# Tree attention over 96 heads: more heads of Q and K laid side by side by GpSimd, with its queue reordered

## The chip, the cores and the metric

The kernel runs on one core of one Trainium2 chip. The metric is device time in microseconds, the median of three runs, and for each profiled kernel one execution was also recorded in full. PE is TensorE's matmul, PEld its weight load, DVE is VectorE, ACT ScalarE, POOL GpSimd, SP SyncE; L364 is line 364 of the kernel.

## The reference, cut to what matters

Batch 8 and 12 heads give 96 heads, each with 512 queries and keys of 64 numbers. A query attends to its own node of a binary tree and to that node's ancestors.

```python
for i in range(seq):
    mask[i, i] = 1
    parent = i
    while parent > 0:
        parent = (parent - 1) // 2
        mask[i, parent] = 1

scores = np.einsum('bhqd,bhkd->bhqk', Q, K) * scale
scores = scores + (1 - mask) * (-1e9)
weights = np.exp(scores - np.max(scores, axis=-1, keepdims=True))
weights = weights / (np.sum(weights, axis=-1, keepdims=True) + 1e-10)
return np.einsum('bhqk,bhkd->bhqd', weights, V).astype(np.float32)
```

## The kernel before

Heads are worked two at a time: 48 pairs, `i` from 0 to 47. Q and K are loaded in blocks of 8 heads (`KB`), V in blocks of 16 (`VB`, called `o` in the code), each load turning fp32 into bf16 on the way. All these loads and most stores are issued by POOL, in the order in which `pool_program` lists them; a store of the last four heads is issued by SP. Each transfer on POOL's queue takes one of eight semaphores in turn, so that POOL waits at an issue until the transfer eight before it has landed.

The first 16 heads use a narrow layout, the other 80 a wide one. In the wide layout a step of K or Q turns two pairs at once: PE transposes 8 slots (`turn_slot`) into PSUM (`ktp`, `qtp`), and DVE copies the result to `kq` (L470, L474, L478 for K, L493 for Q). Where a block is *laid*, POOL has first copied it (`lay`, L433, two copies of 128x512 a block, one for each turn) into `besideK` or `besideQ`, with the two pairs' halves beside each other, and PE needs one transpose a slot (L441). Where it isn't, PE makes two transposes of 64 columns a slot (L450). There is one `besideK` and one `besideQ`, so a lay has to wait for the turn of the laid block before it. `LAID` names the blocks that are laid.

For each pair PE makes scores by matmuls of mask codes and of keys and queries (L511, L519, L544, L554), ACT takes exponentials (L529, L560), PE multiplies them with V (`values`, L605), and DVE divides by the row sums (`norm`, L651 and L653) into the output tile `of`. V has to be rearranged from its load `vst` into three tiles `vt` by copies of 32 to 128 partitions (`spread`, L364). The parts have names: 6 to 9 are the four copies of V's upper rows into `vt0` (`spread_top` when POOL makes all four), X, N, Z0 and Z1 are others from the same rows, A, B, C and E come from the leaves. `BY_VECTOR` and `BY_SCALAR` list which of them DVE and ACT make at which `i`, and `pool_program` lists POOL's.

`store_rows` *deals* the store of the first heads: instead of one store of 128 partitions it issues four, of 85, 2, 34 and 7 partitions (`DEALT`).

`ready` says from which `i` an entry of `pool_program` may be recorded; for a lay it is the turn of the block before in the program. POOL runs its instructions strictly in the recorded order, so what stands behind a waiting one waits too.

Of the kernel before, what the change touches and what calls it, by code (L numbers as in the profile page):

```python
# [119 lines left out]
def kernel(  # L120
# [7 lines left out]
    nc = tc.nc  # L128
# [7 lines left out]
    WIDE = 8  # L136
    KB, VB, VO = 8, 16, 16
    EIGHT = 2
    LAID = (8, 9, 10, 11)
    assert NH % VB == 0  # L140

    fp32 = mybir.dt.float32
# [280 lines left out]
    def slots(st, i):  # L423
        return st[2 * i // KB].rearrange("p (g x) t d -> p g (x t) d", x=2)

    def lay(name, b):

        st = {"kst": ksts, "qst": qsts}[name][b]
        assert all((name, h) in issued for h in range(KB * b, KB * b + KB))
        laid[name, b] = two = beside[name[0].upper()]  # L430
        for g in range(KB // 4):
            src = st[:, 4 * g:4 * g + 4, :, :].rearrange("p (a x) t d -> p (x t) a d", x=2)
            nc.gpsimd.tensor_copy(  # L433
                out=two[:, g, :, :, :].bitcast(int32), in_=src.bitcast(int32)
            )
# [156 lines left out]
    def values(i):  # L592

        if i < NP - 1:
            obs[i] = ob = psO.tile([P, 2, 512], fp32, name="ob")
        else:
            obs[i] = ob = psS.tile([P, 2, 512], fp32, name="s1")
        e1, e2, vt = ets[i], e2s[i % NE], vts[(head(i, 0) // VB) % NV]

        vtile = VTILE if i < WIDE else WVTILE  # L600
        parts = EIGHT_PARTS if head(i, 0) >= VB * EIGHT else PARTS[i >= WIDE]
        assert all(("vt", n, head(i, a)) in issued for n in parts for a in range(2))

        def product(e, a, t, tile_v, lo=0, hi=128, **flags):
            nc.tensor.matmul(  # L605
                out=ob[lo:hi, a, 65 * t:65 * t + 65],
                lhsT=e[:, a, PLACE[t], lo:hi],
                rhs=vt[vtile[tile_v][0]][:, head(i, a) % VB, vtile[tile_v][1], 0:D + 1],
                **flags,
            )  # L610

        def firsts(a):
            for t in range(4):
                product(e1, a, t, 0, start=t == 0, stop=False)

        def halves(a, last=True):
            for t in (0, 1):
                product(e2, a, t, 1 + SELF[t], 0, 64, start=False, stop=last and t == 1)
                product(e2, a, t, 1 + t, 64, 128, start=False, stop=last and t == 1)

        def wholes(a, last=False):
            for t in (2, 3):
                product(e2, a, t, 1 + t, start=False, stop=last and t == 3)

        if i == NP - 1:
            for a in range(2):
                firsts(a)
                wholes(a)
                halves(a)
        elif i >= 4 * LAID[0] - 4:  # L630
            for a in range(2):
                firsts(a)
            for a in range(2):
                halves(a, False)
            for a in range(2):
                wholes(a, True)
        else:
            for a in range(2):
                firsts(a)
                wholes(a)  # L640
            for a in range(2):
                halves(a)
# [28 lines left out]
    def store_rows(j0, j1):  # L671

        for j in range(j0, j1):
            store(nc.gpsimd, 0, 4, 1, DEALT[j], DEALT[j + 1])

    def pool_program():

# [3 lines left out]
            (load_q, 8, 4), (load_v, 8, 8), (load_k, 12, 4),  # L681
            (load_q, 12, 4), (load_k, 16, 8), (load_q, 16, 4), (load_rows, 1, "upper"),
            (load_rows, 1, "even"), (load_rows, 1, "odd"), (load_q, 20, 4),
            (load_k, 24, 8), (load_q, 24, 8), (load_rows, 2, "upper"),
            (load_k, 32, 8), (load_leaves, 2, 0), (load_leaves, 2, 1),
            (load_q, 32, 8), (load_rows, 3, "upper"),
            (spread_pool, (1, "Z0", 8, 16), (1, "Z1", 8, 16)),
            (load_k, 40, 8), (load_q, 40, 8), (load_leaves, 3, 0), (load_leaves, 3, 1),
            (spread_top, 2, 0, 16), (spread_pool, (2, "Z0", 0, 16), (2, "Z1", 0, 16)),
            (load_q, 48, 8), (spread_pool, (2, "X", 0, 16)),  # L690
            (load_k, 48, 8), (spread_pool, (2, "N", 0, 16)),
            (load_rows, 4, "upper"), (spread_top, 3, 0, 16),
            (load_k, 56, 8), (load_q, 56, 8), (load_leaves, 4, 0), (load_leaves, 4, 1),
            (spread_pool, (3, "X", 0, 16), (3, "N", 0, 16), (3, "Z0", 0, 16), (3, "Z1", 0, 16)),
            (load_k, 64, 8), (store_rows, 0, 2), (load_q, 64, 8), (store_rows, 2, 4),
            (load_k, 72, 8), (spread_top, 4), (store, nc.gpsimd, 4, 12), (lay, "kst", 8),
            (load_q, 72, 8), (spread_pool, (4, "X", 0, 16), (4, "N", 0, 16)),
            (lay, "qst", 8), (load_rows, 5, "upper"),
            (spread_pool, (4, "Z0", 0, 16), (4, "Z1", 0, 16)),
            (load_leaves, 5, 0), (load_leaves, 5, 1), (load_k, 80, 8), (load_q, 80, 8),  # L700
            (store, nc.gpsimd, 16, 8), (lay, "kst", 9), (load_k, 88, 8), (load_q, 88, 8),
            (lay, "qst", 9), (store, nc.gpsimd, 24, 8), (store, nc.gpsimd, 32, 16),
            (spread_top, 5), (lay, "kst", 10), (store, nc.gpsimd, 48, 16), (lay, "qst", 10),
# [43 lines left out]
    for o in range(EIGHT, NH // VB):  # L747
# [15 lines left out]
    }  # L763

    def spread_by(copy, table, i):

# [90 lines left out]
```

## Time and profile before

| | us |
|---|---|
| median of three runs (lowest, highest) | 133.66 (133.48, 133.95) |
| the profiled execution's own time | 133.8 |
| its span, from the first to the last instruction | 131.9 |

The engine times of the page count instructions, not waits. Issuing a transfer is an instruction of its queue; a transfer's time to landing includes all that is queued ahead of it. GB/s counts what was written, so a load of fp32 that lands as bf16 counts half of what it read.

| engine | busy us | share of the span |
|---|---|---|
| PE | 114.7 | 87% |
| DVE | 108.8 | 82% |
| ACT | 94.4 | 72% |
| POOL | 87.1 | 66% |

### The profile page before, as it was taken

To read this page: it belongs to the slowest core of one execution; us is meant where nothing else is said; L and a number is where in the kernel's file an instruction comes from. 1 tells how busy PE (TensorE), PEld (TensorE's weight loads), DVE (VectorE), ACT (ScalarE), POOL (GpSimd) and SP (SyncE) were. 2 spreads that over 40 slices of the span, in tenths; PEclk is the share of its full clock that TensorE was granted. 3 is DMA by queue.
4 is the path that set the end of the run, shared out by engine and by line. 5 is a ranking of instruction groups with operands and counts; after the bars stand their busy time and mean duration, and the time that the engine had idled before them with its cause. 6 is when DMAs were issued, how large, how long until landed. Compare 5 with 4: busy or idle time off the path is not lost.

```text
span 131.9 us, 5281 instructions
## 1 busy us (share of the span) xinstructions
PE 114.7 (87%) x2286; PEld 80.4 (61%) x2289; DVE 108.8 (82%) x261; ACT 94.4 (72%) x153; POOL 87.1 (66%) x118
## 2 busy tenths in 40 slices
PE   6883999999789699899899999999988999999920
PEld 2351576676566476666577677677765766776610
DVE  3438569988999989989999999999999999877350
ACT  4358268989768957968858787787868668688900
POOL 6994624245623998799951899999999977802200
PEclk9999599999999999999999999999999999999996
DMA  3999999999999999999999999999999999999984
GB/s 122 216 190 196 198 199 205 199 199 207 206 200 205 204 202 208 209 202 205 202 208 204 244 236 305 338 204 207 203 288 285 228 391 406 400 402 402 397 315 148
DMA packets 29719, 32.28 MB, mean 245 GB/s; under 512 B 1488, under 2 KB 26704, under 8 KB 29696
## 3 DMA queue, kind: packets, MB, share of 16 engines
q0 software_dynamic: 28416, 30.68, 115.2%
q1 hardware_dynamic: 864, 0.93, 2.1%
q10 hardware_dynamic: 416, 0.33, 1.0%
q8 instruction: 18, 0.29, 0.8%
q14 instruction: 5, 0.04, 0.1%
HBM read 37.96 MB, written 12.58 MB: 383 GB/s over the span
## 4 chain that ended last, share of the span: by engine, by line
DVE 38%; PE 24%; DMA 14%; POOL 10%; issue 5%; ACT 3%; ACTq 1%; POOLq 0%
DVE of L653 12%; DVE vt L364 11%; DMA kst<-in_K_dram 8%; PE ob L605 8%; DMA qst<-in_Q_dram 6%; POOL vt L364 5%; DVE rec L651 3%; PE s L511 3%; DVE kq L493 3%; DVE kq L470 3%; DVE kq L478 3%; DVE kq L474 3%; PE s L519 2%; ACT e L560 2%; PE s L544 1%
## 5 line engine op out<-in xcount | busy, mean ns | idle before, releaser
L529 ACT ACTIVATE e<-s 128x1024 bf16<-128x1024 f32 x40 | 40.9, 1023 | 20.7 <-PE s L519 20.1
L605 PE MATMUL ob<-vt,e 128*128 128x65 bf16 (+1 forms) x940 | 39.8, 198 | 6.0 <-DVE of L653 3.0
L605 PEld LDWEIGHTS <-e 128*128 128x128 bf16 (+1 forms) x960 | 31.7, 103 | 15.9 <-DVE of L653 5.1
L560 ACT ACTIVATE e<-s 128x384 bf16<-128x384 f32 x80 | 34.7, 491 | 0.0
L653 DVE TENSOR_TENSOR of<-ob,rec 128x512 f32<-128x512 f32 x47 | 32.5, 691 | 1.6
L364 POOL COPY vt<-vst 32x512 int32<-32x512 int32 (+1 forms) x38 | 31.0, 816 | 2.9 <-PE ob L605 1.2
L364 DVE COPY vt<-vst 32x1024 bf16<-32x1024 bf16 (+6 forms) x54 | 26.8, 497 | 2.3 <-DMA vst<-in_V_dram 1.3
L662 POOL DMA_DIRECT2D out_dram<-of x13 | 12.1, 928 | 12.7 <-DVE of L653 9.2
L511 PE MATMUL s<-codes 40*128 40x512 bf16 x96 | 19.3, 398 | 0.7 <-ACT e L525 0.4
L519 PE MATMUL s<-kq 64*128 64x512 bf16 x96 | 18.5, 380 | 0.0
L651 DVE RECIPROCAL rec<-ob 128x8 f32<-128x8 f32 x47 | 9.6, 204 | 8.8 <-PE ob L605 8.0
L554 PEld LDWEIGHTS <-kq 64*128 64x128 bf16 x320 | 12.1, 94 | 4.8
L554 PE MATMUL s<-kq 64*128 64x160 bf16 (+1 forms) x320 | 14.6, 208 | 0.0
L544 PE MATMUL s<-codes 40*128 40x384 bf16 x80 | 13.6, 333 | 0.3
L493 DVE COPY kq<-qtp 128x1024 bf16<-128x1024 bf16 x20 | 13.6, 681 | 0.0
L256 POOL DMA_DIRECT2D qst<-in_Q_dram x11 | 8.3, 752 | 6.8 <-DMA vst<-in_V_dram 2.6
L525 ACT ACTIVATE e<-s 128x1024 bf16<-128x1024 f32 x8 | 8.2, 1022 | 6.0 <-PE s L519 5.9
L544 PEld LDWEIGHTS <-codes 40*128 40x128 bf16 x80 | 6.1, 94 | 7.9 <-issue 1.2
L256 POOL DMA_DIRECT2D kst<-in_K_dram x10 | 7.6, 760 | 3.9 <-PE ob L605 2.8
L470 DVE COPY kq<-ktp 128x256 bf16<-128x256 bf16 x20 | 8.3, 415 | 0.3 <-PE ktp L450 0.3
L474 DVE COPY kq<-ktp 128x256 bf16<-128x256 bf16 x20 | 8.3, 415 | 0.0
L478 DVE COPY kq<-ktp 128x512 bf16<-128x512 bf16 x20 | 8.3, 414 | 0.0
(49 smaller groups left out, 139.4 us busy)
## 6 DMA issues: line engine op xcount, KB each, us to landing
kst<-in_K_dram POOLq DMA_DIRECT2D x10, 512.0 KB, 13.2
out_dram<-of POOLq DMA_DIRECT2D x5, 1024.0 KB, 13.9
qst<-in_Q_dram POOLq DMA_DIRECT2D x9, 512.0 KB, 14.5
out_dram<-of POOLq DMA_DIRECT2D x2, 2048.0 KB, 20.8
vst<-in_V_dram POOLq DMA_DIRECT2D x12, 256.0 KB, 14.9
vst<-in_V_dram POOLq DMA_DIRECT2D x6, 512.0 KB, 14.3
out_dram<-of POOLq DMA_DIRECT2D x1, 1536.0 KB, 10.7
qst<-in_Q_dram POOLq DMA_DIRECT2D x5, 256.0 KB, 11.9
```

The costliest lines, as they stand in the source:

```text
L256: return nc.gpsimd.dma_start(out=kept[b][:, h0 % KB:h0 % KB + n, :, :].rearrange("p (g x) t d -> p g (x t d)", x=2), in_=wide[:, h0 // 2:( ...
L364: return copy(out=dst, in_=src)
L493: nc.vector.tensor_copy(out=qq[:, :, 0:16, :].rearrange("p b u c -> p b (u c)"), in_=halves)
L511: nc.tensor.matmul(out=sp[:, a, :], lhsT=(k1code if i < WIDE else k1wide)[64 * a:64 * a + CODE_ROWS, :], rhs=(q1code[64 * a:64 * a + CODE_ ...
L519: nc.tensor.matmul(out=sp[:, a, :], lhsT=keys(i, a, TOP), rhs=qTs[i][64 * a:64 * a + 64, :, :].rearrange("p t c -> p (t c)"), start=False, ...
L529: ) if i < WIDE else nc.scalar.activation(
L544: nc.tensor.matmul(out=flat[:, a, :, :].rearrange("p u (t c) -> p u t c", t=4)[:, :, :, 16:64], lhsT=k2wide[64 * a:64 * a + CODE_ROWS, :], ...
L554: nc.tensor.matmul(out=flat[:, a, :, lo:hi], lhsT=keys(i, a, WTILE2[t]), rhs=qT[64 * a:64 * a + 64, :, lo:hi], start=False, stop=t == 1, s ...
L560: nc.scalar.activation(out=e2s[i % NE][:, a, :, 32:128].rearrange("p t (r u) -> p t r u", u=2), in_=flat[:, a, :, :].rearrange("p u (t r) ...
L605: nc.tensor.matmul(out=ob[lo:hi, a, 65 * t:65 * t + 65], lhsT=e[:, a, PLACE[t], lo:hi], rhs=vt[vtile[tile_v][0]][:, head(i, a) % VB, vtile ...
L651: nc.vector.reciprocal(out=rec[:, a:a + n, :, :], in_=o4[:, a:a + n, :, D:D + 1])
L653: nc.vector.tensor_tensor(out=ofs[g][:, first:last + 1:step, :, :], in0=o4[:, a:a + n, :, 0:D], in1=rec[:, a:a + n, :, :].to_broadcast([P, ...
```

## The change

`LAID` gets blocks 2, 3, 4, 5 and 7 (heads 16 to 47 and 56 to 63) beside 8 to 11; block 6 stays as it is. `lay` can make one of its two copies alone. The order of products in `values` was bound to `LAID` and is now bound to `LATE`, with the same value, 28. The four copies of V's upper rows for heads 32 to 63 (`o` of 2 and 3) go from POOL to ACT, one a step, at steps 12 to 15 and 18 to 21. The dealt store holds heads 0 to 2, and the store behind it 13 heads instead of 12. POOL's list is written anew.

```diff
--- before.py
+++ after.py
@@ -136,7 +136,8 @@
     WIDE = 8
     KB, VB, VO = 8, 16, 16
     EIGHT = 2
-    LAID = (8, 9, 10, 11)
+    LAID = (2, 3, 4, 5, 7, 8, 9, 10, 11)
+    LATE = 28
     assert NH % VB == 0
 
     fp32 = mybir.dt.float32
@@ -423,12 +424,12 @@
     def slots(st, i):
         return st[2 * i // KB].rearrange("p (g x) t d -> p g (x t) d", x=2)
 
-    def lay(name, b):
+    def lay(name, b, g0=0, g1=2):
 
         st = {"kst": ksts, "qst": qsts}[name][b]
-        assert all((name, h) in issued for h in range(KB * b, KB * b + KB))
+        assert all((name, h) in issued for h in range(KB * b + 4 * g0, KB * b + 4 * g1))
         laid[name, b] = two = beside[name[0].upper()]
-        for g in range(KB // 4):
+        for g in range(g0, g1):
             src = st[:, 4 * g:4 * g + 4, :, :].rearrange("p (a x) t d -> p (x t) a d", x=2)
             nc.gpsimd.tensor_copy(
                 out=two[:, g, :, :, :].bitcast(int32), in_=src.bitcast(int32)
@@ -627,7 +628,7 @@
                 firsts(a)
                 wholes(a)
                 halves(a)
-        elif i >= 4 * LAID[0] - 4:
+        elif i >= LATE:
             for a in range(2):
                 firsts(a)
             for a in range(2):
@@ -671,7 +672,7 @@
     def store_rows(j0, j1):
 
         for j in range(j0, j1):
-            store(nc.gpsimd, 0, 4, 1, DEALT[j], DEALT[j + 1])
+            store(nc.gpsimd, 0, 3, 1, DEALT[j], DEALT[j + 1])
 
     def pool_program():
 
@@ -681,23 +682,26 @@
             (load_q, 8, 4), (load_v, 8, 8), (load_k, 12, 4),
             (load_q, 12, 4), (load_k, 16, 8), (load_q, 16, 4), (load_rows, 1, "upper"),
             (load_rows, 1, "even"), (load_rows, 1, "odd"), (load_q, 20, 4),
-            (load_k, 24, 8), (load_q, 24, 8), (load_rows, 2, "upper"),
-            (load_k, 32, 8), (load_leaves, 2, 0), (load_leaves, 2, 1),
-            (load_q, 32, 8), (load_rows, 3, "upper"),
-            (spread_pool, (1, "Z0", 8, 16), (1, "Z1", 8, 16)),
-            (load_k, 40, 8), (load_q, 40, 8), (load_leaves, 3, 0), (load_leaves, 3, 1),
-            (spread_top, 2, 0, 16), (spread_pool, (2, "Z0", 0, 16), (2, "Z1", 0, 16)),
-            (load_q, 48, 8), (spread_pool, (2, "X", 0, 16)),
+            (load_k, 24, 8), (load_q, 24, 8), (load_rows, 2, "upper"), (lay, "kst", 2),
+            (load_k, 32, 8), (lay, "qst", 2, 0, 1), (load_leaves, 2, 0), (load_leaves, 2, 1),
+            (load_q, 32, 8), (lay, "qst", 2, 1, 2), (load_rows, 3, "upper"),
+            (spread_pool, (1, "Z0", 8, 16), (1, "Z1", 8, 16)), (lay, "kst", 3),
+            (load_k, 40, 8), (load_q, 40, 8), (lay, "qst", 3),
+            (load_leaves, 3, 0), (load_leaves, 3, 1), (lay, "kst", 4),
+            (spread_pool, (2, "Z0", 0, 16), (2, "Z1", 0, 16), (2, "X", 0, 16)),
+            (load_q, 48, 8), (lay, "qst", 4),
             (load_k, 48, 8), (spread_pool, (2, "N", 0, 16)),
-            (load_rows, 4, "upper"), (spread_top, 3, 0, 16),
-            (load_k, 56, 8), (load_q, 56, 8), (load_leaves, 4, 0), (load_leaves, 4, 1),
+            (load_rows, 4, "upper"), (lay, "kst", 5),
+            (load_k, 56, 8), (load_q, 56, 8), (lay, "qst", 5),
+            (load_leaves, 4, 0), (load_leaves, 4, 1),
             (spread_pool, (3, "X", 0, 16), (3, "N", 0, 16), (3, "Z0", 0, 16), (3, "Z1", 0, 16)),
-            (load_k, 64, 8), (store_rows, 0, 2), (load_q, 64, 8), (store_rows, 2, 4),
-            (load_k, 72, 8), (spread_top, 4), (store, nc.gpsimd, 4, 12), (lay, "kst", 8),
-            (load_q, 72, 8), (spread_pool, (4, "X", 0, 16), (4, "N", 0, 16)),
-            (lay, "qst", 8), (load_rows, 5, "upper"),
+            (load_k, 64, 8), (store_rows, 0, 2), (load_q, 64, 8), (store_rows, 2, 3),
+            (lay, "kst", 7), (store_rows, 3, 4),
+            (load_k, 72, 8), (load_q, 72, 8), (lay, "qst", 7), (spread_top, 4),
+            (store, nc.gpsimd, 3, 13), (spread_pool, (4, "X", 0, 16)), (load_rows, 5, "upper"),
+            (lay, "kst", 8), (spread_pool, (4, "N", 0, 16)), (lay, "qst", 8),
+            (load_leaves, 5, 0), (load_leaves, 5, 1), (load_k, 80, 8), (load_q, 80, 8),
             (spread_pool, (4, "Z0", 0, 16), (4, "Z1", 0, 16)),
-            (load_leaves, 5, 0), (load_leaves, 5, 1), (load_k, 80, 8), (load_q, 80, 8),
             (store, nc.gpsimd, 16, 8), (lay, "kst", 9), (load_k, 88, 8), (load_q, 88, 8),
             (lay, "qst", 9), (store, nc.gpsimd, 24, 8), (store, nc.gpsimd, 32, 16),
             (spread_top, 5), (lay, "kst", 10), (store, nc.gpsimd, 48, 16), (lay, "qst", 10),
@@ -761,6 +765,9 @@
         9: [(1, 6, 8, 16)],
         12: [(1, 9, 8, 16)],
     }
+    for o in (2, 3):
+        for j in range(4):
+            BY_SCALAR.setdefault(6 * o + j, []).append((o, 6 + j, 0, VB))
 
     def spread_by(copy, table, i):
```

The first place is POOL's queue after the load of V's upper rows for heads 32 to 47 (the first row of each piece). `kst` and `qst` are the loaded blocks of K and Q, `besideK` and `besideQ` the laid ones. Before:

```order
L285 DMA vst<-in_V_dram 64x16x256
L256 DMA kst<-in_K_dram 128x4x512
L294 DMA vst<-in_V_dram 32x8x512 x2
L256 DMA qst<-in_Q_dram 128x4x512
L285 DMA vst<-in_V_dram 64x16x256
L364 COPY vt_1_114<-vst 32x16x32 x2
L256 DMA kst<-in_K_dram 128x4x512
L256 DMA qst<-in_Q_dram 128x4x512
L294 DMA vst<-in_V_dram 32x8x512 x2
L364 COPY vt_0_107<-vst 32x16x32 x4
```

And now (line numbers are one higher):

```order
L286 DMA vst<-in_V_dram 64x16x256
L434 COPY besideK<-kst 128x512 x2
L257 DMA kst<-in_K_dram 128x4x512
L434 COPY besideQ<-qst 128x512
L295 DMA vst<-in_V_dram 32x8x512 x2
L257 DMA qst<-in_Q_dram 128x4x512
L434 COPY besideQ<-qst 128x512
L286 DMA vst<-in_V_dram 64x16x256
L365 COPY vt_1_114<-vst 32x16x32 x2
L434 COPY besideK<-kst 128x512 x2
L257 DMA kst<-in_K_dram 128x4x512
L257 DMA qst<-in_Q_dram 128x4x512
```

The transfers keep their order; the lays of K and Q of heads 16 to 23, and of K of 24 to 31, stand between them, and the four copies into `vt_0` are gone from this queue.

The second place is POOL's queue from K of heads 64 to 71 on. `out_dram<-of` are stores. Before:

```order
L256 DMA kst<-in_K_dram 128x4x512
L662 DMA out_dram<-of 85x4x256
L662 DMA out_dram<-of 2x4x256
L256 DMA qst<-in_Q_dram 128x4x512
L662 DMA out_dram<-of 34x4x256
L662 DMA out_dram<-of 7x4x256
L256 DMA kst<-in_K_dram 128x4x512
L364 COPY vt_0_107<-vst 32x16x32 x4
L662 DMA out_dram<-of 128x12x256
L433 COPY besideK<-kst 128x512 x2
L256 DMA qst<-in_Q_dram 128x4x512
L364 COPY vt_2_109<-vst 32x32x32 x2
```

And now:

```order
L257 DMA kst<-in_K_dram 128x4x512
L663 DMA out_dram<-of 85x3x256
L663 DMA out_dram<-of 2x3x256
L257 DMA qst<-in_Q_dram 128x4x512
L663 DMA out_dram<-of 34x3x256
L434 COPY besideK<-kst 128x512 x2
L663 DMA out_dram<-of 7x3x256
L257 DMA kst<-in_K_dram 128x4x512
L257 DMA qst<-in_Q_dram 128x4x512
L434 COPY besideQ<-qst 128x512 x2
L365 COPY vt_0_107<-vst 32x16x32 x4
L663 DMA out_dram<-of 128x13x256
```

Q of heads 72 to 79 follows K of 72 to 79 at once, ahead of the copies and of the wide store; the dealt pieces hold three heads; the lays of block 7 stand among them.

The third place is ACT's queue at steps 12 to 14, each an exponential of 1024 and two of 384 columns. Before:

```order
L364 COPY vt_0_113<-vst 32x8x32
L529 ACTIVATE e_1095<-s_1090 128x1024
L560 ACTIVATE e_1_103<-s_1097 128x4x96 x2
L529 ACTIVATE e_1160<-s_1155 128x1024
L560 ACTIVATE e_2_105<-s_1162 128x4x96 x2
```

And now:

```order
L365 COPY vt_0_113<-vst 32x8x32
L365 COPY vt_0_107<-vst 32x16x32
L530 ACTIVATE e_1040<-s_1035 128x1024
L561 ACTIVATE e_1_103<-s_1042 128x4x96 x2
L365 COPY vt_0_107<-vst 32x16x32
L530 ACTIVATE e_1098<-s_1093 128x1024
L561 ACTIVATE e_2_105<-s_1100 128x4x96 x2
```

A copy into `vt_0` stands behind the exponentials of each step.

## The prediction

> **What bounds the kernel now.** I read the page first, its transfers before its engines.
>
> ```profile
> span 131.9 us, 5281 instructions
> ...
> PE 114.7 (87%) x2286; PEld 80.4 (61%) x2289; DVE 108.8 (82%) x261; ACT 94.4 (72%) x153; POOL 87.1 (66%) x118
> ...
> DMA  3999999999999999999999999999999999999984
> GB/s 122 216 190 196 198 199 205 199 199 207 206 200 205 204 202 208 209 202 205 202 208 204 244 236 305 338 204 207 203 288 285 228 391 406 400 402 402 397 315 148
> ...
> q8 instruction: 18, 0.29, 0.8%
> ...
> HBM read 37.96 MB, written 12.58 MB: 383 GB/s over the span
> ```
>
> The sixteen DMA engines are at 90% or more in all slices but the first and the last two. A load reads fp32 and writes bf16, so 205 GB/s written there are 410 read, as fast as the stores' 400 at the end. 50.5 MB at 405 GB/s take 125 us of a span of 131.9: the kernel ends when its transfers do, and only the ends are open. So next the tail: windows (busy us by engine, granted clock, DMA share, GB/s), the issues from 127.0 on, and the last two stores.
>
> ```profile
> 123.00:126.00 3.00, 2.87 (x58) 1.95 (x55) 1.76 (x4) 2.31 (x5) 0.76 (x1) 1.00 1.00 396
> ...
> 127.00:128.00 1.00, 0.00 (x0) 0.00 (x0) 0.39 (x1) 0.00 (x0) 0.00 (x0) 1.00 0.57 217
> 128.00:129.00 1.00, 0.00 (x0) 0.00 (x0) 0.00 (x0) 0.00 (x0) 0.00 (x0) 1.00 0.80 295
> 129.00:130.00 1.00, 0.00 (x0) 0.00 (x0) 0.00 (x0) 0.00 (x0) 0.00 (x0) 0.73 0.89 314
> 130.00:131.00 1.00, 0.00 (x0) 0.00 (x0) 0.00 (x0) 0.00 (x0) 0.00 (x0) 0.50 0.11 38
> ```
> ```profile
> q1 hardware_dynamic: 528, 0.52, 30.2%
> q0 software_dynamic: 104, 0.34, 18.2%
> ...
> out_dram<-of SPq DMA_DIRECT2D x1, 512.0 KB, 3.6
> ```
> ```profile
> 124.42 0.76 POOL L662 DMA_DIRECT2D out_dram<-of  x1 [3.42 <-DVE of L653]
> ...
> 127.41 0.39 SPq L662 DMA_DIRECT2D out_dram<-of  x1
> ```
> ```profile
> out_dram<-of POOLq DMA_DIRECT2D x1, 512.0 KB, 5.3
> ```
>
> The last four heads leave at 127.41 and land 3.6 us later, at 131.0; 0.9 us of end follow. The store before them leaves at 124.42 and lands 5.3 us later, at 129.7, though from 127 to 128 the engines are at 0.57 in the mean: some are through while others are two microseconds behind. From 127.0 to 131.9, POOL's stores (q0) still hold 18.2% of 4.9 us, that is 0.89 us of all engines. **Two things end together**: the slowest DMA engine, and the compute, without which SP cannot issue. In a row of transfers with no gap, an earlier compute gives the slowest engine nothing.
>
> What paces the compute stands in the chain of waits (start, us, what) and in the groups by form.
>
> ```profile
> 39.18 0.45 PE qtp L450 x16
> ...
> 43.69 0.45 PE qtp L450 x16
> ...
> 49.05 0.90 DVE vt L364
> ...
> 74.56 0.69 DVE vt L364
> ...
> 110.61 0.70 DVE of L653
> ...
> 112.25 0.45 PE ktp L441 x8
> ```
> ```profile
> L364 DVE COPY vt<-vst 32x1024 bf16<-32x1024 bf16 x36 | 19.6, 543 | 1.9 <-DMA vst<-in_V_dram 1.3
> ...
> L364 POOL COPY vt<-vst 32x1024 int32<-32x1024 int32 x16 | 17.3, 1078 | 0.7
> ...
> L364 POOL COPY vt<-vst 32x512 int32<-32x512 int32 x22 | 13.8, 626 | 2.2 <-PE ob L605 1.2
> ...
> L433 POOL COPY besideQ<-qst 128x512 int32<-128x512 int32 x8 | 5.3, 680 | 0.2
> ...
> L433 POOL COPY besideK<-kst 128x512 int32<-128x512 int32 x8 | 4.7, 612 | 1.1 <-PE ktp L441 0.9
> ...
> L364 ACT COPY vt<-vst 32x512 int32<-32x512 int32 x3 | 1.8, 616 | 0.1
> ```
>
> From 74.56 to 110.61 the chain runs on DVE without a break, then on PE. So DVE time counts up to 111 us, and POOL's and ACT's only where they hold DVE or a transfer up.
>
> **The change part by part.** *Turns.* A laid slot takes one transpose where an unlaid one takes two: 8 against 16 a turn. The two PE rows of the chain give 0.45 us for either, so the path gains nothing. What goes is instructions: 5 blocks x 2 names x 2 turns x 8 = 160 transposes, and as many weight loads, 320 of PE's 4575 (x2286 and x2289 on the page).
>
> *Instruction transfers.* The q8 row has 18 packets of 0.29 MB, 16 KB each, and 0.29 MB over 4575 instructions is 64 B each, so they are PE's program. 320 instructions are 20.5 KB, 1.25 packets: one or two fewer. What one costs is in the window from 119 to 123 us, which has one:
>
> ```profile
> q8 instruction: 1, 0.02, 1.6%
> ```
>
> 1.6% of sixteen engines for 4 us is 1.02 us, on a single engine. The end gains between 0 (that engine is not the last) and 1.02 us. The Trainium skill, in "Runtime: NRT & Kernel Launch", Instruction fetch mechanics, says that instructions come in blocks of 16 KiB, 256 at a time, and that their fetching is mostly hidden. The sizes agree with the q8 row; by the page alone nothing would be gained, which is the first rival.
>
> *Dealt store.* Four pieces shrink from 512 KB together to 384, and the store behind them grows from 1536 to 1664: no byte is added, a quarter of the dealing's unevenness goes. Which engine carries what no view shows. Bounds for the two DMA terms together: the end cannot gain more than the 0.89 us of q0 that stand in the way of SP's store after 127.0, and it loses the growth of the other store, 128 KB / 400 GB/s = 0.3 us, if the engines that get more are the last. I take half of the gain, **-0.45 us**, since the likeliest last engines are those that fetch or those that were dealt most, and both get less. The Trainium skill, in "DMA: Bandwidth & Descriptors", Why a DMA increments its semaphore by 16 and not by 1, says that a transfer uses the largest number up to 16 that divides its rows, and that such groups follow each other round. By it 85, 2, 34 and 7 rows are 5, 2, 2 and 7 engines, sixteen in all, seven with 17 rows each and nine with one; those seven would lose 17 KB and gain 8 of the wider store, an estimate of 0.36 us at 25 GB/s an engine. No row here shows the engines.
>
> *POOL's copies.* 20 lay copies come (10 lays of two) and 8 of the 32x512 form go to ACT: 20 x 0.646 - 8 x 0.626 = +7.9 us on an engine at 66%. Their price is paid by DVE:
>
> ```profile
> L364 DVE COPY vt<-vst x41: 220/422/1054, 27.4 to 109.5; 32x1024 bf16<-32x1024 bf16 x30, 32x512 bf16<-32x512 bf16 x5, 128x1024 bf16<-128x1024 bf16 x2, 64x1024 bf16<-64x1024 bf16 x2
> ...
> 48.64 1.03 POOL L364 COPY vt<-vst 32x1024 int32<-32x1024 int32 x1
> ```
>
> The same DVE copy takes 422 ns in the median and up to 1054. The one of 0.90 in the chain ends at 49.95, after a POOL copy that ran from 48.64 to 49.67: it stood behind it. The excess over the median is 36 x (543 - 422) = 4.4 us. A copy that finds POOL busy waits for what is left of POOL's instruction, so the excess goes with count times length squared: before, 16 x 1.08² + 22 x 0.63² + 16 x 0.65² = 34; after, 16 x 1.08² + 14 x 0.63² + 36 x 0.65² = 39, 15% more, **+0.67 us on DVE**. Bounds: 0, if the new copies fall between DVE's; +3.1 us, if half of the 20 each cost what the chain's copy lost (0.90 - 0.42 = 0.48), less the 8 at the mean rate of 4.4 / 54 = 0.08 us and DVE's idle time (0.7 us of the ten from 50 on, row below), another 1 us or so. I take +0.45, a third of the 0.67 lost in idle time. The compute may come 0.45 us later without harm if q0 is 0.45 us sooner: SP's store then starts behind an emptier queue (0.89 - 0.45 = 0.44 left).
>
> *ACT's copies.*
>
> ```profile
> 50.00:60.00 10.00, 9.04 (x210) 6.49 (x209) 9.29 (x23) 7.20 (x13) 8.58 (x12) 1.00 1.24 206
> ```
> ```profile
> L529 ACT ACTIVATE e<-s 128x1024 bf16<-128x1024 f32 x40 | 40.9, 1023 | 20.7 <-PE s L519 20.1
> ```
>
> 8 x 0.616 = 4.9 us, one copy a step over eight steps; the cover is ACT's wait for scores, 20.7 us over 40 steps, 0.5 us a step, and ACT idles 2.8 us of these ten. So 0.1 us a step can reach the next exponential, which its products need a step later: nothing. With no cover, 0.6 us a step, 4.9 in all.
>
> *POOL's order.* The lays stand ahead of loads and can make them late:
>
> ```profile
> 37.63 0.74 POOL L256 DMA_DIRECT2D qst<-in_Q_dram  x1 [1.99 <-PE ktp L450]
> ...
> 78.59 0.76 POOL L256 DMA_DIRECT2D qst<-in_Q_dram  x1
> ...
> 83.00 0.84 POOL L285 DMA_DIRECT2D vst<-in_V_dram  x1
> ...
> kst<-in_K_dram POOLq DMA_DIRECT2D x10, 512.0 KB, 13.2
> ```
>
> A load lands 13.2 us after its issue and moves in 2.5 us (1 MB read at 410 GB/s), so 10 us of work wait ahead of it; a lay of 1.3 us ahead costs nothing. Q of 72 moves up from 78.59 to behind K of 72, some 4.5 us, and V's upper rows of 80 from 83.00 to about 80.7; the store of the first 16 goes back by two. Nothing waits for that store but its buffer. The lays' own waits: a second copy needs the turn two back, long done. The tightest is Q of 24: its lay follows the issue at 37.63, 38.4 + 0.68 = 39.1, against a turn at 39.2. If it misses, PE's turn and DVE's copy of it come late by as much; I take none.
>
> **Sum**, against the profiled execution's 133.8 us (131.9 and 1.9 around): -0.45 at the last engine, +0.45 of compute hidden behind it: 133.35. The median of the runs, 133.66, lies 0.14 below that execution, so **133.2 us**; its own range 132.8 to 133.4.
>
> **The rivals.** *The end stays.* The engine that ends last is neither one that fetches nor one that was dealt more, or the compute eats the gain: -0.45 in the sum becomes -0.15 to +0.15, 133.5 to 133.8. For it: only one engine in sixteen carries a given packet. Against: the engines differ by some 2 us, so few can be the last. 0.3% of 133.66 is 0.4 us, about what a measurement of this kernel can tell from no change. *DVE stands behind the lays* (slower). Laying Q and K of 16 to 47 puts ten lays between 24 and 75 us, where before POOL only spread V. If they cost DVE 2 us, SP issues at 129.4, and only 0.89 us of that is covered by the drained queue: +1.1 us, 134.8. It decides from 0.9 us on. For it: the chain's 0.90, and nothing on DVE is removed; against: the mean excess is 0.12 us a copy. *POOL starves the transfers.* A lay that waits for a late load would hold the loads behind it; every microsecond of empty engines is one at the end, 1 to 2 us, 135. Against: 10 us of queue.
>
> **How the numbers follow.** Forecast 0.42; the end stays 0.22; DVE behind the lays 0.31; starved 0.05. Faster 0.42, same 0.22, slower 0.36. The range takes the forecast, the second and most of the third: 132.7 to 134.8.
>
> **What would show it.** Right: 16 or 17 packets in q8, PE with 4255 instructions or so, the last POOL store landing closer to 4.9 than to 5.3 us after its issue, SP's issue before 127.9, a DVE copy of 32x1024 at 545 to 565 ns in the mean. Wrong: SP's issue later than 128.3, DVE's copies over 600 ns, a DMA share under 1.0 before 120 us, or q0's share after SP's issue unchanged.

## The result, and the profile after

The changed kernel takes 134.78 us (median of 15 runs, 133.76 to 137.21) against 133.66 for the kernel before beside it (133.28 to 134.15). The ratio is 1.0081, with a 95% interval from 1.0061 to 1.0102: **slower by 0.8%**. Predicted were 133.2 us and, as likelier than slower, faster. Executions that took over 1.5% more than the fastest of their kernel are left out of all ratios and readings, three profiled ones among them (the second of the upper copies alone, block 7 in the old order, the first with ten copies moved).

The page of the changed kernel, in the order in which that of before was read (profiled execution 135.04 us):

```profile
span 133.3 us, 4979 instructions
...
PE 116.4 (87%) x2126; PEld 81.5 (61%) x2129; DVE 111.2 (83%) x261; ACT 99.0 (74%) x161; POOL 94.8 (71%) x130
...
q8 instruction: 16, 0.26, 0.7%
...
HBM read 37.96 MB, written 12.58 MB: 379 GB/s over the span
...
DVE 51%; PE 23%; ACT 7%; issue 6%; DMA 6%; POOL 3%; ACTq 1%; POOLq 0%
```

PE has 2126 + 2129 = 4255 instructions and q8 16 packets, two fewer than before. The last row is the chain of waits by engine. Before, it read:

```profile
DVE 38%; PE 24%; DMA 14%; POOL 10%; issue 5%; ACT 3%; ACTq 1%; POOLq 0%
```

DMA's share of this chain falls from 14% to 6% and DVE's grows by 13 points. The tail, in the same columns as that of before (windows, then POOL's last store and SP's, then what these two took to land):

```profile
127.00:128.00 1.00, 0.93 (x20) 0.69 (x20) 0.72 (x2) 0.73 (x2) 0.32 (x1) 1.00 0.22 86
128.00:129.00 1.00, 0.29 (x8) 0.14 (x4) 0.81 (x4) 0.00 (x0) 0.00 (x0) 1.00 1.00 414
129.00:130.00 1.00, 0.00 (x0) 0.00 (x0) 0.49 (x2) 0.00 (x0) 0.00 (x0) 0.59 0.17 66
130.00:131.00 1.00, 0.00 (x0) 0.00 (x0) 0.00 (x0) 0.00 (x0) 0.00 (x0) 0.50 0.53 189
```
```profile
126.56 0.77 POOL L663 DMA_DIRECT2D out_dram<-of  x1 [3.41 <-DVE of L654]
...
129.55 0.39 SPq L663 DMA_DIRECT2D out_dram<-of  x1
```
```profile
out_dram<-of POOLq DMA_DIRECT2D x1, 512.0 KB, 3.2
out_dram<-of SPq DMA_DIRECT2D x1, 512.0 KB, 2.8
```

From 127 to 128 us the DMA engines are at 0.22 and from 129 to 130 at 0.17: they have nothing left to move. SP's store, issued at 129.55, finds them empty and lands in 2.8 us; the span ends 3.75 us after its issue (133.3 - 129.55), where before it ended 4.5 us after it (131.9 - 127.41). So the transfers no longer hold the end. The compute does, and it comes **2.1 us later** than before (SP's issue at 129.55 against 127.41).

Where DVE lost it is seen in the groups by form, of after:

```profile
L365 DVE COPY vt<-vst 32x1024 bf16<-32x1024 bf16 x36 | 20.9, 580 | 1.9 <-DMA vst<-in_V_dram 1.2
...
L365 POOL COPY vt<-vst 32x1024 int32<-32x1024 int32 x16 | 17.3, 1081 | 0.8
...
L434 POOL COPY besideQ<-qst 128x512 int32<-128x512 int32 x18 | 11.5, 663 | 0.2
```

and in the windows restricted to the line of the V copies (busy us of DVE, ACT, POOL, with counts), first of before, then of after:

```profile
24.00:48.00 24.00, 6.31 (x14) 3.27 (x7) 5.79 (x8) 1.00 1.33 202
...
sum 89.00, DVE 22.04 ACT 3.27 POOL 29.07; mean DVE 5.51 ACT 0.82 POOL 7.27
```
```profile
24.00:48.00 24.00, 8.53 (x14) 3.63 (x8) 4.43 (x5) 1.00 1.33 203
...
sum 89.00, DVE 24.66 ACT 7.65 POOL 23.55; mean DVE 6.16 ACT 1.91 POOL 5.89
```

The same 14 copies of DVE take 2.2 us more between 24 and 48 us, and the copies from 24 to 113 us take 2.6 us more in all. Two places show how. At 24 us, DVE before and after:

```profile
25.21 0.41 DVE L364 COPY vt<-vst 32x1024 bf16<-32x1024 bf16 x1
...
27.38 0.22 DVE L364 COPY vt<-vst 32x256 bf16<-32x256 bf16 x1
```
```profile
24.83 0.87 DVE L365 COPY vt<-vst 32x1024 bf16<-32x1024 bf16 x1
...
27.39 0.51 DVE L365 COPY vt<-vst 32x256 bf16<-32x256 bf16 x1
```

and POOL after, at the same time:

```profile
24.81 1.36 POOL L434 COPY besideK<-kst 128x512 int32<-128x512 int32 x2
26.43 0.76 POOL L257 DMA_DIRECT2D kst<-in_K_dram  x1 [0.26 <-PE ob L606]
27.18 0.62 POOL L434 COPY besideQ<-qst 128x512 int32<-128x512 int32 x1
```

Before, POOL was not copying there, and DVE's copies took their bare 0.41 and 0.22 us. Now a new lay runs when each starts: the second ends at 27.90, 0.10 us after the lay's end at 27.80. At 44 us it is V's long copies, which have no short copies of the upper rows ahead of them any more and run three in a row (POOL, then the chain of waits):

```profile
44.37 3.30 POOL L365 COPY vt<-vst 32x1024 int32<-32x1024 int32 x3
```
```profile
44.41 1.27 DVE vt L365
...
45.70 1.03 DVE vt L365
```

These two take 2.3 us together; before, in the same place behind the short copies, they took 1.4.

### The profile page after: what moved, and what is told of

Its sections match the earlier page's. It is cut to its first block, busy times and chain, and to the rows that moved or that the text cites. A ratio compares the mean times of both kernels' runs of the same rounds, so it can differ in the third digit from the quotient of the medians.

```text
span 133.3 us, 4979 instructions
## 1 busy us (share of the span) xinstructions
PE 116.4 (87%) x2126; PEld 81.5 (61%) x2129; DVE 111.2 (83%) x261; ACT 99.0 (74%) x161; POOL 94.8 (71%) x130
## 4 chain that ended last, share of the span: by engine, by line
DVE 51%; PE 23%; ACT 7%; issue 6%; DMA 6%; POOL 3%; ACTq 1%; POOLq 0%
DVE of L654 16%; DVE vt L365 16%; PE ob L606 10%; DMA qst<-in_Q_dram 6%; DVE rec L652 5%; DVE kq L494 4%; ACT e L561 4%; DVE kq L471 3%; DVE kq L479 3%; DVE kq L475 3%; PE s L512 3%; PE ktp L442 2%; ACT e L530 2%; PE s L520 2%; ACT vt L365 2%
## 5 line engine op out<-in xcount | busy, mean ns | idle before, releaser
L530 ACT ACTIVATE e<-s 128x1024 bf16<-128x1024 f32 x40 | 40.9, 1024 | 18.1 <-PE s L520 17.1
L365 DVE COPY vt<-vst 32x1024 bf16<-32x1024 bf16 (+6 forms) x54 | 29.4, 544 | 2.2 <-DMA vst<-in_V_dram 1.2
L365 POOL COPY vt<-vst 32x1024 int32<-32x1024 int32 (+1 forms) x30 | 26.0, 866 | 1.5
L434 POOL COPY besideK<-kst 128x512 int32<-128x512 int32 x18 | 11.5, 656 | 3.0 <-PE ktp L442 2.1
L365 ACT COPY vt<-vst 32x512 int32<-32x512 int32 (+3 forms) x21 | 11.1, 529 | 1.0 <-DMA vst<-in_V_dram 0.6
L434 POOL COPY besideQ<-qst 128x512 int32<-128x512 int32 x18 | 11.5, 663 | 0.2
L442 PE MATMUL ktp<-ptile,besideK 128*128 128x128 bf16 x144 | 11.1, 219 | 0.3 <-DVE kq L479 0.3
L442 PE MATMUL qtp<-ptile,besideQ 128*128 128x128 bf16 x144 | 11.1, 219 | 0.0
## 6 DMA issues: line engine op xcount, KB each, us to landing
out_dram<-of POOLq DMA_DIRECT2D x5, 1024.0 KB, 12.3
```

What stands on the lines that cost most here:

```text
L365: return copy(out=dst, in_=src)
L434: nc.gpsimd.tensor_copy(out=two[:, g, :, :, :].bitcast(int32), in_=src.bitcast(int32))
L442: nc.tensor.transpose(out=out(dst), in_=two[:, 2 * i % KB // 4, s, :, :].rearrange("p a d -> p (a d)"), identity=ptile[:, 0:128],)
L530: ) if i < WIDE else nc.scalar.activation(
```

## The experiments

Two numbers are read from each profile: when SP issues the last store, and what DVE's copies of V take from 24 to 113 us (the sum above). The bare duration of such a copy is 0.42 us (0.28 or 0.22 for the smaller forms); what is over is called held. Each is read from one execution, so they scatter: in the kernel before and in two that have its POOL queue up to 60 us, the second number is 22.0, 23.3 and 22.8 us.

**Each part of the change alone.** *The dealt store*, in the kernel before: `store(nc.gpsimd, 0, 3, ...)` and `(store, nc.gpsimd, 3, 13)`.

> The kernel before with one part of the change, heads 0 to 2 dealt. No compute moves: SP's issue stays at 127.4. Theory, the dealing offsets the instruction transfers of PE, of which there are still 18: a quarter less of it leaves the last engine where it is or up to 0.3 us later, 133.6 to 134.0 us. Rival, the dealt engines were the last: 0.4 us sooner, 133.2.

Measured 133.67 us, 1.001 (0.9991 to 1.003); SP's issue at 127.39, span 131.8, DVE 23.27 us. The dealt store alone is worth nothing that can be measured.

*The upper copies by ACT*, in the kernel before:

```diff
-            (spread_top, 2, 0, 16), (spread_pool, (2, "Z0", 0, 16), (2, "Z1", 0, 16)),
+            (spread_pool, (2, "Z0", 0, 16), (2, "Z1", 0, 16)),
-            (load_rows, 4, "upper"), (spread_top, 3, 0, 16),
+            (load_rows, 4, "upper"),
+    for o in (2, 3):
+        for j in range(4):
+            BY_SCALAR.setdefault(6 * o + j, []).append((o, 6 + j, 0, VB))
```

> The kernel before with one part of the change: the four upper copies of heads 32 to 63 by ScalarE, POOL's eight short copies gone; no new lays, old order, dealt as before. The kernel without new lays took 134.02 us (1.0031 of before), so some part other than the lays costs about 0.4 us. Theory 'ACT's copies are covered by its waits': SP's last issue at 127.4 within 0.5, time 133.2 to 133.6, ratio 0.998 to 1.002. Rival 'ACT's copies make exponentials late': eight copies of 0.6 us, uncovered in part, SP's issue at 128.2 or later, time 133.9 to 134.2, ratio 1.003 or more.

Measured 133.72 us, 1.0001 (0.9987 to 1.0014); SP's issue at 125.61, DVE 20.61 us, span 131.5. ACT's copies cost nothing that can be measured. In this profile the compute is 1.8 us earlier than before without any gain: the span ends 5.9 us after SP's issue. This is the transfers' own end. The same kernel once more:

> The tops-alone kernel once more, word for word, for a second profile. Theory 'its lead is of the order': SP's issue within 0.4 us of 125.60, DVE's copies held for 4 to 5.5 us. Rival 'phase': SP's issue at 126.5 to 128.5, held 6 to 8 us.

This execution took 136.18 us and is one of the three left out, so it gives no answer.

*POOL's later order*, in the kernel before (the list from K of 72 on as in the change, without the lays of block 7).

> The kernel before with only POOL's order from Q of 72 on as in the change (Q of 72 right behind K of 72, V's upper rows of 80 and the leaves, K and Q of 80 sooner, the copies Z0 and Z1 of 64 behind them); no new lays, tops on POOL, dealt as before. Theory 'order costs nothing, transfers have 10 us of queue': SP's issue at 127.4 within 0.5, 18 instruction packets, time 133.2 to 133.6, ratio 0.998 to 1.002. Rival 'the moved copies meet DVE's or the store that waits holds what is behind it': SP's issue at 128 or later, time 133.9 or more.

Measured 133.63 us, 1.0009 (0.9993 to 1.0024); SP's issue at 127.33, DVE 22.77 us. The order alone costs nothing that can be measured.

*The change without its new lays* (`LAID = (8, 9, 10, 11)`, the ten new `lay` entries out of POOL's list):

> The changed kernel with only blocks 8 to 11 laid, as before; the rest of the change stays (four upper copies of heads 32 to 63 on ACT, Q of 72 sooner, heads 0 to 2 dealt). Theory, DVE stands behind POOL's copies: the lays between 24 and 43 us cost DVE 0.6 us (pair 8's division at 37.6 instead of 38.2 us), but the long copies into vt, which come first now that the four short ones are gone from POOL, still meet DVE at 44 to 46 us; SP's last issue at 127.9 to 128.5 (127.4 before, 129.5 changed), 133.7 to 134.3 us. Rival, the lays alone are the cost: SP's issue at 127.4, 133.7. Rival, ACT's copies are the cost: as the changed kernel, 134.8. q8 back at 18 packets in all.

Measured 134.02 us, 1.0031 (1.0009 to 1.0054), 18 packets; SP's issue at 128.45, DVE 24.15 us. So the lays are not all of it: the other three parts, each free by itself, together end the compute 1 us later than before in this profile, with DVE's copies held nearly as long as in the change (8.0 us from 24 us on, against 8.1).

**The lays.** *The change without the lays of heads 16 to 31* (`LAID = (4, 5, 7, 8, ...)`):

> The change with the lays of heads 16 to 31 left away again (heads 32 to 47 and 56 to 63 laid). Those eight lay copies at 24 to 36 us stood ahead of DVE copies that lost 0.45, 0.22, 0.32, 0.1 and 0.3 us. Theory 'these early lays set the end by what DVE lost there': SP's last issue 0.6 us or more before the change's, at 128.9 or sooner, 17 instruction packets, time 133.9 to 134.2. Rival 'an early lead is lost again by 80 us, as in the run with the dealt store alone': SP's issue 129.3 or later, time 134.4 to 134.9, as with the change.

Measured 134.36 us, 1.005 (1.0031 to 1.0069), 17 packets; SP's issue at 128.96, DVE 23.15 us (five runs). The time is between the change and the kernel without new lays, and the intervals overlap both. The early loss is gone, but a new one stands at 47 us: PE waits 1.9 us for the lay of Q of 32 to 39, which comes late in a crowded queue of POOL's.

*The change with the upper copies back on POOL* (`spread_top` of 2 and 3 in POOL's list again):

> The changed kernel with the eight upper copies of heads 32 to 63 back on POOL, ahead of the copies that they stood ahead of before. Theory, DVE stands behind POOL's copies: POOL has 5 us more of copies, so no gain, 134.5 to 135.3 us, SP's issue at 129.3 or later. Rival, ACT's copies delay the exponentials: back to 133.5 to 133.9 us and SP's issue at 127.5 to 128.

Measured 138.93 us, 1.039 (1.0351 to 1.043). Its waits (us in total, times, longest), then POOL at 44 us:

```profile
PEld L442 <- POOL besideQ L434: 4.8, 5, 2.6
PE qtp L442 <- POOL besideQ L434: 4.2, 5, 2.5
```
```profile
44.17 5.97 POOL L365 COPY vt<-vst 32x512 int32<-32x512 int32 x7
...
50.90 1.16 POOL L434 COPY besideQ<-qst 128x512 int32<-128x512 int32 x2
```

The time is 3.6 us above the most that was expected. DVE's copies are held no longer than in the change. What costs here is another thing: seven copies stand ahead of the lay, and PE's turn waits for it. ACT's taking the copies is what makes room for the lays.

**What holds DVE.** *POOL's long copies in halves* (each 32x1024 copy as two of 32x512), in the change:

> The changed kernel with POOL's copies of 32x1024 into vt made as two of 32x512 each. Theory, a DVE copy waits for the rest of the POOL instruction in progress: the longest DVE copies fall from 1.27 to some 0.8 us, their sum by 1.5 to 2 us, SP's issue at 127.7 to 128.2, 133.0 to 133.6 us, faster than before too, since q8 has 16 packets. Rival, the time that POOL holds DVE off goes with POOL's busy time: 14 copies more of 0.2 us each make it 0.2 to 0.5 us slower, 135.

Measured 134.38 us, 1.0071 (1.0045 to 1.0097); SP's issue at 128.52, DVE 24.63 us. Shorter instructions give shorter holds, but no smaller sum: counted copy by copy in the trace, 32 of DVE's 41 copies are held by over 0.03 us, for 8.5 us, where in the change 22 of 42 are, for 8.1. Count times length squared, by which the prediction priced the holds, goes from 39 to 33 (the 18.7 of the long copies becomes 32 x 0.62² = 12.3), a sixth less. By that pricing 8.1 us would have become 6.8; the 8.5 speaks against it, though single profiles of one POOL queue differ by over 1 us.

*Eight of POOL's long copies left out* (`Z0`, `Z1`, `X`, `N` of heads 32 to 63), in the change:

> The change, with POOL's eight 32x1024 copies of heads 32 to 63 (Z0, Z1, X, N) left out, so part of V's rows is not laid out; everything else as it is. Theory 'POOL's copies hold DVE's': in the change the DVE copies at 44.4, 45.7, 50.5 and 62.5 us stood 0.86, 0.75, 0.72 and 0.38 us behind them, 2.7 us together; without them these take 0.28 to 0.55 us, the span from pair 8 to pair 17 shrinks from 22.9 to 20.8 us or less, SP's last issue comes at 127.9 or sooner, and the time is 132.9 to 133.5. Rival 'PE's turns and ACT's copies pace the compute there': pair 8 to 17 stays at 22.5 to 23.2 us, time 134.4 to 134.9.

Measured 133.67 us (133.38 over the eight executions of twelve that count), 0.9982 (0.9963 to 1.0000); SP's issue at 127.62, DVE 23.02 us. The stretch from the division of pair 8 to that of pair 17 takes 21.3 us (22.9 in the change), and DVE's copies are held for 1.0 us in it (2.7 in the change). So POOL's copies hold DVE up by 1.7 us there; the rival, that PE and ACT pace it, falls. That is a little less than expected (20.8 us or less); the gain in time is as expected.

**Place or phase.** In the kernel without new lays and in the change, the copy `X` of heads 32 to 47 was put back behind the load of Q of 48:

> The kernel of e1_no_new_lays (tops by ScalarE, later order, dealt 3, no new lays; 134.02 us, SP's issue at 128.44) with one swap: POOL's copy X of heads 32 to 47 behind the load of Q of 48, as in the kernel before, not ahead of it. The tops alone, with that order, issued SP's store at 125.60 and the late order alone and the dealt store alone cost nothing. Theory 'three long copies in a row meet DVE's copies at 42 to 46 us and make Q of 48 late': with the swap SP's issue comes at 126.2 or sooner, DVE's vt copies sum to 27 us or less (29.1 in e1), time 133.2 to 133.6, held by the transfers with their 18 instruction packets. Rival 'e1's loss is chance of phase, not this swap': SP's issue 127.5 or later, time 133.7 to 134.1.

> The change with one swap: POOL's copy X of heads 32 to 47 behind the load of Q of 48 and its lay of Q of 32, not ahead of them. Theory 'the loss between pair 8 and 13 (14.5 us in the before's own place 12.5) is made by the three copies in a row': pair 8 to 13 takes 13.0 us or less (13.55 in the change, 12.51 before), SP's issue 0.7 us or more before the change's 129.54, time 133.2 to 134.2. Rival 'POOL's copies cost by their number, wherever they stand': SP's issue 129.2 or later, time 134.4 to 134.9, DVE's vt copies 29 us or more.

Measured 133.72 us, 1.0013 (0.9987 to 1.0039), SP's issue at 128.60, DVE 23.69 us; and 134.56 us, 1.0077 (1.0048 to 1.0107), SP's issue at 129.14, DVE 24.10 us. The swap moves neither compute by more than 0.4 us. The first runs the same instructions up to 64 us, on PE, DVE, ACT and POOL, as the tops alone, yet it issues SP's store 3 us later. The three us are there by pair 17, at 60 us, so no edit made them: they differ between executions. The change once more, for a second profile:

> The changed kernel once more, word for word, for a second profile. Theory 'the change's lays set the loss': SP's issue within 0.6 us of 129.54, DVE's copies from pair 4 to 12 held for 3 us or more (3.68 in the first profile, 1.45 to 2.2 in the kernels without lays there). Rival 'phase': either number elsewhere, SP's issue below 128.5.

134.69 us, SP's issue at 129.21, DVE 23.96 us. The end is where it was, though the loss fell elsewhere: its copies from pair 4 to 12 were held for about 2 us only (over 3 in the first profile), those behind them for longer. And in this profile PE waits for lays, which it never does in the first: 1.8 us in three turns, for Q of heads 16, 24 and 32 (at 27, 39 and 49 us).

```profile
PEld L442 <- POOL besideQ L434: 1.8, 3, 0.7
PE qtp L442 <- POOL besideQ L434: 1.5, 3, 0.6
```

Two things in the traces tell what differs between executions. One is the granted clock in 40 slices of the span, in tenths, of before, of the change's two profiles and of the tops alone:

```profile
PEclk9999599999999999999999999999999999999996
PEclk9999599999999999999999999999999999999985
PEclk9999999999999999999999999999999999999996
PEclk9999999999999999999999999999999999999965
```

In the first two it falls to 0.68 and 0.64 in the mean from 12 to 16 us, and pair 5 is divided 1.4 us or so later than in the other two. So before and the first profile of the change compare like with like (2.1 us at SP's issue), and so do the second and the dealt store alone, which have no dip (129.21 against 127.39: 1.8 us). `X` put back without lays has one too (0.73), which is 0.9 of its 3 us behind the tops alone.

The other is the stretch from the division of pair 8 to that of pair 13, set beside the time for which DVE's copies in it are held:

| profile | pair 8 to 13, us | held, us | rest, us |
|---|---|---|---|
| before | 12.51 | 1.28 | 11.23 |
| the change | 13.56 | 2.33 | 11.22 |
| the change, second profile | 11.92 | 0.67 | 11.25 |
| its eight long copies left out | 12.05 | 0.83 | 11.22 |
| tops alone | 11.22 | 0.01 | 11.21 |
| `X` put back, no new lays | 12.52 | 1.30 | 11.22 |
| tops and block 7 (below) | 12.94 | 1.72 | 11.22 |

What is left without the holds is the same in all, 11.21 to 11.25 us, so here every microsecond of a hold is one of the compute. The last three rows run the same instructions up to there and are held for 0.0, 1.3 and 1.7 us: the lead of the tops alone was the luck of one execution. From pair 5 to 46 the first profile of the change takes 2.1 us more than before and is held for 1.9 more; the second takes 2.0 more than the dealt store alone and is held for 1.1 more, and about 0.7 of what remains is PE's waiting for the lays: pair 5 to 8 and pair 13 to 17, less their holds, are longer by 0.3 and 0.4 us there.

**Versions put together.** The free parts with the lays of block 7 alone, in the later and in the old order:

> A version put together from the parts that cost nothing: tops of heads 32 to 63 by ScalarE, X behind the load of Q of 48, the later order, dealt 3, and of the new lays only heads 56 to 63 (64 of PE's instructions fewer). Theory 'the compute has then 1.5 us of lead and the transfers set the end': SP's issue at 126.5 or sooner, 17 instruction packets, all engines through between 129.5 and 130.4, time 132.7 to 133.3, faster than before by 0.2 to 0.6%. Rival 'one packet fewer moves nothing, since the last engine is another': 133.3 to 133.7.

> The kernel before with the tops of heads 32 to 63 by ScalarE, the lays of heads 56 to 63 and dealt 3, in POOL's old order (without the later order of the change). Theory 'the lead of the tops alone (SP's issue at 125.60) is of the order and stays': SP's issue at 127.0 or sooner, 17 instruction packets, time 132.8 to 133.3, faster than before by 0.2 to 0.6%. Rival 'where DVE's copies meet POOL's is a matter of phase, which any edit shifts': SP's issue anywhere from 127.3 to 129, DVE's vt copies held for 6 to 8.5 us in all (4.5 in the tops alone), time 133.5 to 134.4.

Measured 134.35 us, 1.0052 (1.0024 to 1.008), SP's issue at 128.69, DVE 24.20 us; and 135.58 us (134.93 over the nine executions that count), 1.0093 (1.0054 to 1.0131). Both are slower than before; there was no lead of the tops alone to carry over.

**DVE's own work taken away.** Six, then ten of DVE's 36 copies of 32x1024 go to ACT:

```diff
+    for i in (17, 23, 27, 31, 35, 39):
+        BY_SCALAR.setdefault(i, []).append(BY_VECTOR[i].pop())
```

> The change with six of DVE's 36 copies of leaves (one every four steps or so, from step 17 to 39) made by ScalarE. Theory 'DVE with its held copies paces the compute, and the change's transfers end sooner': each copy off DVE frees 0.42 us and the 0.2 us for which it is held in the mean, 3.7 us in all; SP's last issue at 126 to 127.6 (129.54 and 129.20 in the change), transfers then set the end with their 16 instruction packets, time 132.6 to 133.4, faster than before by 0.2 to 0.8%. Rival 'PE and ACT are as late as DVE': ACT's copies of 0.6 us come out of waits of 0.4 us a step, SP's issue at 129 or later, time 134.4 to 135.

> The kernel before with the same six copies made by ScalarE, nothing else. Theory 'the transfers alone then hold the end, with 18 packets': SP's issue at 124 to 126, the store's last engine at 130 to 131 all the same, time 133.2 to 133.5, ratio 0.997 to 1.000. Rival 'the compute sets the end of the kernel before': time follows SP's issue down to 131.5 to 132.8. Rival 'PE and ACT are as late': SP's issue at 127.3 or later, time 133.5 or more.

> The change with ten of DVE's copies of leaves made by ScalarE (step 17 and every other step from 23 to 39). Theory 'DVE paces': SP's issue at 125 to 127, earlier than with six, time 132.5 to 133.3. Rival 'ACT paces from some number on': ACT is then busy for 105 us and its exponentials come late, SP's issue no earlier than with six, 127.5 or later, time 133.4 or more.

In the change, six: **133.27 us, 0.9965 (0.995 to 0.998)**. In the kernel before, six: 133.62 us, 0.9998 (0.9983 to 1.0012). In the change, ten: 132.97 us over the five executions that count, 0.9944 (0.9929 to 0.996). The span, the chain and SP's issue, of six in the change and of six in the kernel before:

```profile
span 131.5 us, 4983 instructions
...
PE 57%; DVE 17%; ACT 10%; DMA 5%; issue 4%; POOL 3%; ACTq 1%; POOLq 0%
...
127.77 0.39 SPq L663 DMA_DIRECT2D out_dram<-of  x1
```
```profile
span 131.6 us, 5288 instructions
...
PE 55%; DVE 24%; DMA 6%; issue 4%; POOL 3%; ACT 3%; ACTq 1%; POOLq 0%
...
126.02 0.39 SPq L662 DMA_DIRECT2D out_dram<-of  x1
```

In the change, SP's issue is 1.4 to 1.8 us sooner than without the edit and the time follows. In the kernel before, SP's issue is also 1.4 us sooner, and the span is 131.6 against 131.9: the transfers hold the end there. Taking work off DVE paid in the change, where the compute held the end, and not in the kernel before, where the transfers did. Ten copies once more:

> The change with ten copies by ScalarE once more, word for word, for its timeline and a second set of times (133.02 us, 0.9944 of before in the first). Theory 'DVE paces, and the compute now ends at or before the transfers': SP's issue at 127.3 or sooner, DVE's copies of leaves 23 us or less in all, the chain of waits mostly PE, time 132.7 to 133.3, ratio 0.992 to 0.997. Rival 'the first set was luck of phase': time 133.4 or more.

Measured 133.39 us, 0.9998 (0.9966 to 1.0029), 12 runs; SP's issue at 126.96, span 131.4, DVE 19.16 us. The second set doesn't bear out the first. What the three sets show is that the change is mended (133.0 to 133.4 against 134.8); a gain of about 0.3% over the kernel before is shown for six copies in one set, and for ten it stays open.

## Why the prediction was wrong

*What bounds the kernel: right.* Two things end together. Where SP issues at 127.4 or sooner, the kernels with 18 packets all have spans of 131.5 to 131.9 us: issues at 127.41, 127.39, 127.33, 126.02, 125.61 end 4.4 to 5.9 us later. Where the compute is the later one, the end follows the issue by 3.7 us, in all eleven such profiles (127.62 to 131.3 without the long copies, 127.77 to 131.5 with six copies moved, 129.55 to 133.3 in the change). So before, the compute had 131.8 - 127.4 - 3.7 = 0.7 us to lose; the prediction had 0.9.

*The transfers: right in kind, the size is open.* 16 packets and 4255 instructions came as said. The change's transfers can be read only where the compute is out of the way: with ten copies moved, the span is 131.4 with SP's issue at 126.96, some 0.3 us under the 131.7 which is the mean of the five spans above, and 0.1 under the shortest. Predicted were 0.45; one profile doesn't settle the size. How much of it is packets and how much the dealt store isn't settled; the dealt store alone showed nothing.

*Turns, ACT's copies, the loads' order: right.* PE's transposes are 219 ns in the mean with 16 or 8 a turn, the tops alone took 1.0001 and the order alone 1.0009.

*The lays' own waits: put at nothing, and not nothing.* The prediction saw that the lay of Q of 24 was tight and took none for it. In the first profile of the change nobody waited; in the second PE waited for it and for the lays of Q of 16 and 32, 1.8 us in all, of which about 0.7 reached the compute. Two variants show more (1.9 and 4.8 us of PE's waiting).

*POOL's copies: this is the step that failed.* The prediction saw that a DVE copy that finds POOL at work waits for the rest of POOL's instruction, and named it. It priced it at count times length squared, +15% of 4.4 us, **+0.67 on DVE and +0.45 on the compute**, "hidden behind" the transfers' -0.45. Measured: DVE's copies from 24 to 113 us took 24.66 and 23.96 us in the two profiles of the change, 24.3 in the mean, against 22.04, 23.27 and 22.77 in the kernel before and the two that have its POOL queue up to 60 us, 22.7 in the mean: **+1.6 us on DVE**, and **+2.0 at SP's issue** (129.4 against 127.4). Of this 0.7 was covered and 1.3 was not: 131.8 + 1.3 = 133.1, against spans of 133.3 and 132.9.

Three things were wrong in the price. It let a third of the loss vanish in DVE's idle time; in the table above, none vanishes. It took the excess of one form of copy in one profile (4.4 us) as the whole, where the held time over all forms is 5.5, 6.7 and 6.5 us in the three profiles named, and 8.1 and 7.8 in the change. And it let this grow by 15%, as if POOL's instructions met DVE's at random, where it grew by 27%; halving POOL's long copies did not lower it. Why it grew by more is not shown.

*The second rival is what came.* *DVE stands behind the lays* ("If they cost DVE 2 us, SP issues at 129.4", and 134.8 us) was given 0.31; the issue was at 129.55 and 129.21, and the time 134.78. Only its cause was too narrow. The lays are a part of it: with the new lays the ratio goes from 1.0031 to 1.0081, and from 1.0013 to 1.0077 with `X` put back, 0.7 to 0.9 us. The rest, about 1 us at SP's issue, is there without them (128.45, 128.60), when the upper copies have left POOL, its order is changed and the store is dealt in threes, none of which costs anything alone. DVE's copies are held for longer there too (24.15 and 23.69 us). The tops alone show that part of this is the execution's luck; whether one of the three parts also brings more meetings stays open.

*The signs.* The mean of a DVE copy was to be 545 to 565 ns if right and over 600 if wrong; 580 is neither. SP's issue later than 128.3 was named as proof against, and came. POOL's last store was to land 4.9 us after its issue; 3.2 shows drained engines, not balanced ones, and no packet of POOL's queue was left after SP's issue.

The Trainium skill, in "SBUF — State Buffer", Who interferes with whom, says that VectorE's copies between SBUF operands in their fast modes and GpSimd share one pair of ports, and that whoever issues first keeps it for the whole instruction. The traces agree: of DVE's work from 24 us on only the copies `vt<-vst`, from SBUF to SBUF, stretch (0.40 to 1.27 us for the form of 32x1024), while those from PSUM do not (679 to 683 ns each in this row; the groups by form, of before and of after):

```profile
L493 DVE COPY kq<-qtp 128x1024 bf16<-128x1024 bf16 x20 | 13.6, 681 | 0.0
```
```profile
L494 DVE COPY kq<-qtp 128x1024 bf16<-128x1024 bf16 x20 | 13.6, 680 | 0.0
```
By that page the hold is the rest of POOL's instruction, which is what the prediction took; it gives no rule for how often it happens, and there the prediction went wrong.

## What to carry to other kernels

Where a second engine holds up the engine that paces, price a new instruction there by the hold that a trace shows next to it (0.3 to 0.9 us here), not by a mean over the kernel, and take off nothing for idle time before a trace shows it; two profiles of the kernel as it is tell how far such a sum scatters. Subtract the holds from the time of a stretch: if the rest is the same in every kernel, they are the cause, and what is left over is another wait. Where transfers and compute end together, an edit that helps the one at the other's cost is worth nothing until the other has slack: first make the room (copies off DVE), then spend it. Spans against the last issue tell which of the two ends a kernel: a constant distance means compute, a constant end means transfers.

## What the runs showed of the hardware

GpSimd's issuing of a transfer holds DVE's copy too, not its copies alone. The longest hold of the kernel before ends 0.22 us after the issue of a store (DVE in the chain of waits, then POOL):

```profile
99.84 1.05 DVE vt L364
```
```profile
99.52 1.15 POOL L662 DMA_DIRECT2D out_dram<-of  x1
```

Of the 5.5 us for which DVE's copies from 24 us on are held in the kernel before, 2.0 us are behind POOL's issues and 3.5 behind its copies (from the trace, copy by copy). And halving POOL's copies does not halve the hold: in the two profiles 0.37 us a held copy became 0.27, but 22 of them became 32.
